# Eight experts on one core: x in two large loads, stores on the gpsimd ring, the last two gated to a weight piece

## The chip, the cores and the metric

The kernel runs on one core of a Trainium2 chip. The metric is the device time of one execution in microseconds, as the median of several runs. TensorE multiplies; VectorE (DVE) and ScalarE (ACT) empty its accumulators; GpSimd (POOL) and SyncE (SP) here mostly issue transfers. A transfer is carried by the core's 16 DMA engines, whichever engine issued it. Transfers issued by gpsimd and those issued by sync or scalar stand in different queues, called rings below. A transfer that changes the type (float32 to bfloat16) is issued by gpsimd in this kernel.

## What is computed

```
x:  8 experts x 256 rows x 512      w1: 8 x 512 x 2048      w2: 8 x 2048 x 512   (float32)
h = max(x @ w1, 0)
out = h @ w2                         8 x 256 x 512 float32
```

Each expert has two weights of 4.19 MB in float32. The 16 of them, 67.1 MB, are read once; x and the output are 4.19 MB each.

## The kernel before

All matmuls run in bfloat16. Weights are cast on the way in: each is one gpsimd DMA (L57 for w1, L63 for w2) into a tile of 128 partitions x 8192 elements, that is 32 KB of float32 in a row of DRAM per partition and 16 KB of bfloat16 in SBUF. The pool "weights" has four buffers for w1 and four for w2 (both are called w_sb in the profile). The w2 of the last two experts come in pieces: three for expert 6, seven for expert 7, the last three of them one k-slice each.

x comes expert by expert in float32 on the sync queue (L53): 128 partitions x 2 rows of 512, 4 KB per partition. Four experts are loaded ahead; expert e + 4 is loaded after the second layer of e. ACT casts it (L67), TensorE transposes it in eight 128x128 blocks (L73), and DVE evicts the blocks (L77). Cast and transposes of expert e + 1 stand inside the first layer of expert e.

A first layer is 64 matmuls per expert (L89) into eight accumulators, each emptied with a relu by DVE (L97) or ACT (L99) into ht. A second layer is 32 matmuls (L111) into two accumulators of 128x512, evicted by DVE (L119) and ACT (L120) into an output tile. The store of an expert is one 0.5 MB DMA on the sync queue (L125), as soon as both evictions are done; the last expert's goes out in two halves, on sync (L122) and scalar (L123).

The order is written out by hand: first and second layer of experts 0 to 4 in turn, then the first layers of 5, 6, 7, then their second layers. Weights are issued in the order of use, all from the gpsimd queue, which works in order: a weight whose buffer is still in use holds up everything behind it. A transfer on the gpsimd ring also waits for the eighth before it, since their completion is counted on eight semaphores in rotation.

Of the kernel before, what the change touches and what calls it, by code (L numbers as in the profile page):

```python
# [1 line left out]

# [5 lines left out]


@with_exitstack  # L10
def kernel(
    ctx: ExitStack,
    tc: tile.TileContext,
    x: bass.AP,
    w1: bass.AP,
    w2: bass.AP,
    out: bass.AP,
):
    nc = tc.nc
    P = 128  # L20
    bf = mybir.dt.bfloat16
    f32 = mybir.dt.float32

    E, C, H = x.shape
    F = w1.shape[2]
    MT = C // P
    KT1 = H // P
    KT2 = F // P
    AHEAD = 4


    x_r = x.rearrange("e (p mt) k -> e p mt k", p=P)
    w1_r = w1.rearrange("e (p kt) n -> e p kt n", p=P)
    w2_r = w2.rearrange("e (p kt) n -> e p kt n", p=P)
    out_r = out.rearrange("e (p mt) n -> e p mt n", p=P)

    const = ctx.enter_context(tc.tile_pool(name="const", bufs=1))
    wpool = ctx.enter_context(tc.tile_pool(name="weights", bufs=4))
    xpool = ctx.enter_context(tc.tile_pool(name="xs", bufs=AHEAD))
    tpool = ctx.enter_context(tc.tile_pool(name="xts", bufs=2))  # L40
    hpool = ctx.enter_context(tc.tile_pool(name="hidden", bufs=4))
    opool = ctx.enter_context(tc.tile_pool(name="outs", bufs=3))
    ps_h = ctx.enter_context(tc.tile_pool(name="ps_h", bufs=4, space=bass.MemoryType.PSUM))
    ps_o = ctx.enter_context(tc.tile_pool(name="ps_o", bufs=4, space=bass.MemoryType.PSUM))

    x_sb, xb, xt, w1_sb, w2_sb, ht = {}, {}, {}, {}, {}, {}


    ctx.enter_context(tc.manual_schedule())

    def load_x(e):
        x_sb[e] = xpool.tile([P, MT, H], f32, tag="x", name="x_sb")
        nc.sync.dma_start(x_sb[e][:], x_r[e])  # L53

    def load_w1(e):
        w1_sb[e] = wpool.tile([P, KT1, F], bf, tag="w1", name="w1_sb")
        nc.gpsimd.dma_start(w1_sb[e][:], w1_r[e])  # L57

    def load_w2(e):
        w2_sb[e] = wpool.tile([P, KT2, H], bf, tag="w2", name="w2_sb")  # L60
        cuts = {E - 2: (0, 6, 11, 16), E - 1: (0, 4, 8, 11, 13, 14, 15, 16)}.get(e, (0, KT2))
        for lo, hi in zip(cuts, cuts[1:]):
            nc.gpsimd.dma_start(w2_sb[e][:, lo:hi, :], w2_r[e, :, lo:hi, :])  # L63

    def cast_x(e):
        xb[e] = tpool.tile([P, MT, H], bf, tag="xb", name="x_bf")
        nc.scalar.copy(xb[e][:], x_sb[e][:])  # L67

    def transpose_x(e):
        pt = ps_o.tile([P, KT1, MT, P], bf, tag="ps_o", name="pt_tr")  # L70
        for kt in range(KT1):
            for mt in range(MT):
                nc.tensor.transpose(  # L73
                    pt[:, kt, mt, :], xb[e][:, mt, kt::KT1], identity[:]
                )
        xt[e] = tpool.tile([P, KT1, C], bf, tag="xt", name="xt_sb")
        nc.vector.tensor_copy(xt[e][:], pt[:].rearrange("p k m q -> p k (m q)"))  # L77

    def first_layer(e):
        if e + 1 < E:  # L80
            cast_x(e + 1)
        ht[e] = hpool.tile([P, KT2, C], bf, tag="ht", name="ht_sb")
        for g in range(KT2 // 2):
            if g == KT2 // 4 and e + 1 < E:
                transpose_x(e + 1)
            ph = ps_h.tile([P, 2, C], f32, tag="ps_h", name="pt_h")
            for i in range(2):
                for kt in range(KT1):
                    nc.tensor.matmul(  # L89
                        ph[:, i, :],  # L90
                        w1_sb[e][:, kt, 2 * g + i::KT2],
                        xt[e][:, kt, :],
                        start=(kt == 0),
                        stop=(kt == KT1 - 1),
                    )
            if g % 2:
                nc.vector.tensor_relu(ht[e][:, 2 * g:2 * g + 2, :], ph[:])  # L97
            else:
                nc.scalar.activation(  # L99
                    ht[e][:, 2 * g:2 * g + 2, :], ph[:],  # L100
                    mybir.ActivationFunctionType.Relu,
                )

    def second_layer(e):
        last = e == E - 1
        po = [
            ps_o.tile([P, H], f32, tag="ps_o", name=f"pt_o{mt}") for mt in range(MT)
        ]
        order = [(kt, mt) for kt in range(KT2) for mt in range(MT)]
        for kt, mt in order:  # L110
            nc.tensor.matmul(  # L111
                po[mt][:],
                ht[e][:, kt, mt * P:(mt + 1) * P],
                w2_sb[e][:, kt, :],
                start=(kt == 0),
                stop=(kt == KT2 - 1),
            )
        o = opool.tile([P, MT, H], f32, tag="o", name="out_sb")
        nc.vector.tensor_copy(o[:, 0, :], po[0][:])  # L119
        nc.scalar.copy(o[:, 1, :], po[1][:])  # L120
        if last:
            nc.sync.dma_start(out_r[e, :, 0, :], o[:, 0, :])  # L122
            nc.scalar.dma_start(out_r[e, :, 1, :], o[:, 1, :])  # L123
        else:
            nc.sync.dma_start(out_r[e], o[:])  # L125


    order = []
    for e in range(E - 3):
        order += [(1, e), (2, e)]  # L130
    order += [(1, e) for e in range(E - 3, E)] + [(2, e) for e in range(E - 3, E)]

    for e in range(AHEAD):
        load_x(e)
    for layer, e in order:
        (load_w1 if layer == 1 else load_w2)(e)
        if (layer, e) == (1, 0):
            identity = const.tile([P, P], bf, name="identity")
            make_identity(nc, identity)
    cast_x(0)  # L140
    transpose_x(0)
    for layer, e in order:
        if layer == 1:
            first_layer(e)
        else:
            second_layer(e)
            if e + AHEAD < E:
                load_x(e + AHEAD)


# [1 line left out]
_INS = ['x', 'w1', 'w2']  # L152
_OUTS = [((8, 256, 512), 'float32')]


# [23 lines left out]
```

## Time and profile before

| | |
|---|---|
| time, median of three (lowest, highest) | 185.76 us (185.62, 185.86) |
| span of the profiled run | 183.9 us |
| mean granted TensorE clock | 0.924 |
| gpsimd ring: packets, MB written | 3456, 33.56 |
| sync ring: packets, MB written | 2304, 8.13 |
| scalar ring: packets, MB written | 144, 0.26 |
| median from issue to landing: x load, store, 2 MB weight | 26.1, 16.1, 65.1 us |

The page of a profile has the busy time of each engine, a picture of the span in 40 slices, the DMA queues, the chain of work that ended last, the groups of instructions by line with what ended the idle time before them, and the DMA issues. The MB of a queue count what is written, so a weight that is read as 4.19 MB counts as 2.10 MB. Time of idle on an engine that is not the bottleneck costs nothing.

### The profile page before, as it was taken

To read this page: it belongs to the slowest core of one execution; us is meant where nothing else is said; L and a number is where in the kernel's file an instruction comes from. 1 tells how busy PE (TensorE), PEld (TensorE's weight loads), DVE (VectorE), ACT (ScalarE), POOL (GpSimd) and SP (SyncE) were. 2 spreads that over 40 slices of the span, in tenths; PEclk is the share of its full clock that TensorE was granted. 3 is DMA by queue.
4 is the path that set the end of the run, shared out by engine and by line. 5 is a ranking of instruction groups with operands and counts; after the bars stand their busy time and mean duration, and the time that the engine had idled before them with its cause. 6 is when DMAs were issued, how large, how long until landed. Compare 5 with 4: busy or idle time off the path is not lost.

```text
span 183.9 us, 1901 instructions
## 1 busy us (share of the span) xinstructions
PE 132.1 (72%) x832; PEld 91.9 (50%) x832; DVE 32.5 (18%) x48; ACT 32.8 (18%) x49; POOL 13.5 (7%) x30
## 2 busy tenths in 40 slices
PE   0204959579891996929987396865989595899980
PEld 0103954159640892317942385324889494344420
DVE  0100430104301141001411033010244333010101
ACT  3300220312103130021302212031143132010101
POOL 7300010100100001000040100101010010210000
PEclk9999999957999699985999979996699999999999
DMA  5999999989999999999999999999999999999973
GB/s 221 274 217 219 280 214 228 224 201 232 265 215 246 251 219 248 246 217 257 249 212 254 236 223 272 216 224 274 215 232 214 228 228 190 212 214 240 232 190 116
DMA packets 5912, 42.06 MB, mean 229 GB/s; under 512 B 656, under 2 KB 1040, under 8 KB 4112
## 3 DMA queue, kind: packets, MB, share of 16 engines
q0 software_dynamic: 3456, 33.56, 86.4%
q1 hardware_dynamic: 2304, 8.13, 11.7%
q10 hardware_dynamic: 144, 0.26, 0.4%
q8 instruction: 6, 0.10, 0.2%
q14 instruction: 2, 0.02, 0.0%
HBM read 71.30 MB, written 4.19 MB: 410 GB/s over the span
## 4 chain that ended last, share of the span: by engine, by line
another core or an unknown queue 38%; DMA 33%; PE 19%; POOL 4%; issue 3%; DVE 0%; POOLq 0%
DMA w_sb<-in_w_dram 33%; PE pt_h L89 10%; PE pt_o L111 8%; POOL w_sb L63 3%; POOL w_sb L57 1%; PE pt_tr L73 0%; DVE out_sb L119 0%; POOL identity masks.py:199 0%; POOL identity masks.py:197 0%; POOLq masks.py:199 0%; POOLq L174 0%; POOLq L63 0%; POOLq L163 0%
## 5 line engine op out<-in xcount | busy, mean ns | idle before, releaser
L89 PE MATMUL pt_h<-xt_sb,w_sb 128*128 128x256 bf16 x512 | 72.1, 310 | 31.2 <-DMA w_sb<-in_w_dram 31.2
L89 PEld LDWEIGHTS <-w_sb 128*128 128x128 bf16 x512 | 63.1, 150 | 40.3 <-DMA w_sb<-in_w_dram 34.4
L111 PE MATMUL pt_o<-w_sb,ht_sb 128*128 128x512 bf16 x256 | 57.0, 379 | 11.0 <-DMA w_sb<-in_w_dram 10.9
L111 PEld LDWEIGHTS <-ht_sb 128*128 128x128 bf16 x256 | 25.0, 98 | 41.6 <-issue 13.4
L97 DVE TENSOR_SCALAR ht_sb<-pt_h 128x512 bf16<-128x512 f32 x32 | 22.1, 692 | 80.0 <-PE pt_h L89 80.0
L99 ACT ACTIVATE ht_sb<-pt_h 128x512 bf16<-128x512 f32 x32 | 19.1, 597 | 75.9 <-PE pt_h L89 75.9
L120 ACT COPY out_sb<-pt_o 128x512 f32<-128x512 f32 x8 | 4.7, 586 | 68.5 <-PE pt_o L111 68.5
L119 DVE COPY out_sb<-pt_o 128x512 f32<-128x512 f32 x8 | 5.5, 691 | 61.7 <-PE pt_o L111 61.7
L63 POOL DMA_DIRECT2D w_sb<-in_w_dram x16 | 8.6, 540 | 73.6 <-DMA w_sb<-in_w_dram 65.1
L57 POOL DMA_DIRECT2D w_sb<-in_w_dram x8 | 4.4, 556 | 76.7 <-PE pt_h L89 75.9
L73 PE MATMUL pt_tr<-identity,x_bf 128*128 128x128 bf16 x64 | 5.3, 230 | 5.2 <-ACT x_bf L67 5.2
L67 ACT CAST x_bf<-x_sb 128x1024 bf16<-128x1024 f32 x8 | 8.4, 1046 | 2.3 <-DMA x_sb<-in_x_dram 2.3
L73 PEld LDWEIGHTS <-x_bf 128*128 128x128 bf16 x64 | 4.7, 116 | 5.2 <-ACT x_bf L67 5.2
L77 DVE COPY xt_sb<-pt_tr 128x1024 bf16<-128x1024 bf16 x8 | 5.5, 682 | 6.3 <-PE pt_tr L73 6.3
L67 ACT ACT_TABLE_LOAD x1 | 1.3, 1283 | 0.7 <-PEq L163 0.7
masks.py:199 POOL TENSOR_SCALAR_AFFINE_SELECT identity<-identity 128x128 bf16<-128x128 bf16 x1 | 0.3, 288 | 0.1
masks.py:197 POOL MEMSET identity<- 128x128 bf16 x1 | 0.2, 223 | 0.0
L163 POOL MEMSET const-float32-0.0<- 128x1 f32 x1 | 0.1, 98 | 0.2 <-issue 0.2
L163 POOL MEMSET const-bfloat16-1.0<- 128x1 bf16 x1 | 0.1, 102 | 0.0
L163 POOL MEMSET const-uint8-127<- 128x1 uint8 x1 | 0.1, 102 | 0.0
L163 POOL MEMSET const-float32-1.0<- 128x1 f32 x1 | 0.1, 98 | 0.0
## 6 DMA issues: line engine op xcount, KB each, us to landing
w_sb<-in_w_dram POOLq DMA_DIRECT2D x14, 2048.0 KB, 65.1
x_sb<-in_x_dram SPq DMA_DIRECT2D x8, 512.0 KB, 26.1
out_dram<-out_sb SPq DMA_DIRECT2D x7, 512.0 KB, 16.1
w_sb<-in_w_dram POOLq DMA_DIRECT2D x2, 640.0 KB, 65.6
w_sb<-in_w_dram POOLq DMA_DIRECT2D x2, 512.0 KB, 49.6
w_sb<-in_w_dram POOLq DMA_DIRECT2D x1, 768.0 KB, 66.6
w_sb<-in_w_dram POOLq DMA_DIRECT2D x1, 384.0 KB, 37.1
w_sb<-in_w_dram POOLq DMA_DIRECT2D x3, 128.0 KB, 17.8
```

Of the source, the lines that this page charges most:

```text
L57: nc.gpsimd.dma_start(w1_sb[e][:], w1_r[e])
L63: nc.gpsimd.dma_start(w2_sb[e][:, lo:hi, :], w2_r[e, :, lo:hi, :])
L67: nc.scalar.copy(xb[e][:], x_sb[e][:])
L73: nc.tensor.transpose(pt[:, kt, mt, :], xb[e][:, mt, kt::KT1], identity[:])
L77: nc.vector.tensor_copy(xt[e][:], pt[:].rearrange("p k m q -> p k (m q)"))
L89: nc.tensor.matmul(ph[:, i, :], w1_sb[e][:, kt, 2 * g + i::KT2], xt[e][:, kt, :], start=(kt == 0), stop=(kt == KT1 - 1),)
L97: nc.vector.tensor_relu(ht[e][:, 2 * g:2 * g + 2, :], ph[:])
L99: nc.scalar.activation(ht[e][:, 2 * g:2 * g + 2, :], ph[:], mybir.ActivationFunctionType.Relu,)
L111: nc.tensor.matmul(po[mt][:], ht[e][:, kt, mt * P:(mt + 1) * P], w2_sb[e][:, kt, :], start=(kt == 0), stop=(kt == KT2 - 1),)
L119: nc.vector.tensor_copy(o[:, 0, :], po[0][:])
L120: nc.scalar.copy(o[:, 1, :], po[1][:])
L163: nc = _bacc.Bacc("TRN2", target_bir_lowering=False, num_devices=1)
```

## The change

x is read in two loads of four experts each, with eight rows of 512 (16 KB) per partition. The first comes in float32 on the sync queue and is cast by ACT in four pieces; the second is cast on the way by a gpsimd DMA that stands between the weights of expert 1. Each group is transposed at once: the first before any matmul, the second inside the first layer of expert 2, a quarter after every second accumulator. Since partition p now holds eight successive rows, the eviction of the transposes puts columns back in order with a strided pattern, shared between DVE and ACT.

The weights get three buffers of each kind instead of four, which makes room for the x tiles and five output tiles.

The stores of experts 0 to 4 are issued by gpsimd, each at a place chosen among the weights; the queue then carries, in order: w1 3, w2 3, store 0, w1 4, w2 4, store 1, w1 5, w1 6, w1 7, w2 5, store 2, w2 6, store 3, store 4, w2 7. The stores of 5 and 6 stay on sync, but wait until the third last piece of the last weight has landed; they are meant to keep out of the way of the last weights. The stores on gpsimd and the long rows of x are meant to keep small packets from standing between those of the weights.

```diff
-    AHEAD = 4
-    x_r = x.rearrange("e (p mt) k -> e p mt k", p=P)
+    G = 2
+    EG = E // G
+    J = EG * C // P
+    WB = 3
+    x_r = x.rearrange("(g e) c k -> g (e c) k", g=G).rearrange(
+        "g (p j) k -> g p j k", p=P
+    )
...
-    wpool = ctx.enter_context(tc.tile_pool(name="weights", bufs=4))
+    wpool = ctx.enter_context(tc.tile_pool(name="weights", bufs=WB))
+    hpool = ctx.enter_context(tc.tile_pool(name="hidden", bufs=3))
+    opool = ctx.enter_context(tc.tile_pool(name="outs", bufs=5))
...
+    def transpose_x(g, kts):
+        for kt in kts:
+            pt = ps_o.tile([P, J, P], bf, tag="ps_o", name="pt_tr")
+            for j in range(J):
+                nc.tensor.transpose(pt[:, j, :], x_b[g][:, j, kt::KT1], identity[:])
...
+                if mt % 2:
+                    nc.scalar.copy(dst, src[:, mt])
+                else:
+                    nc.vector.tensor_copy(dst, src[:, mt])
...
+    def store(e):
+        nc.gpsimd.dma_start(out_r[e], o_sb[e][:])
+
+    nc.sync.dma_start(x_f[:], x_r[0])
+    load_w1(0)
+    make_identity(nc, identity)
+    load_w2(0)
+    load_w1(1)
+    nc.gpsimd.dma_start(x_b[1][:], x_r[1])
+    load_w2(1)
+    load_w1(2)
+    load_w2(2)
+    for j in range(0, J, 2):
+        nc.scalar.copy(x_b[0][:, j:j + 2, :], x_f[:, j:j + 2, :])
+    transpose_x(0, range(KT1))
+
+    first_layer(0)
+    load_w1(3)
+    second_layer(0)
+    load_w2(3)
+    store(0)
+    first_layer(1)
+    load_w1(4)
+    second_layer(1)
+    load_w2(4)
+    store(1)
+    first_layer(2, [lambda kt=kt: transpose_x(1, [kt]) for kt in range(KT1)])
+    load_w1(5)
+    second_layer(2)
+    first_layer(3)
+    load_w1(6)
+    second_layer(3)
+    first_layer(4)
+    load_w1(7)
+    load_w2(5)
+    store(2)
+    load_w2(6)
+    store(3)
+    second_layer(4)
+    store(4)
+    load_w2(7)
...
+    for e in (5, 6):
+        d = nc.sync.dma_start(out_r[e], o_sb[e][:])
+        tc.add_manual_dep(
+            d.ins,
+            pieces[-3].ins.name,
...
+            reason="after the weights",
+        )
+    nc.sync.dma_start(out_r[7, :, 0, :], o_sb[7][:, 0, :])
+    nc.scalar.dma_start(out_r[7, :, 1, :], o_sb[7][:, 1, :])
```

## The prediction

> **What bounds the kernel now.** I read the page from the engine shares to the queues, then the TensorE timeline, then the DMA answers for single stretches. On the page, TensorE is busy 72% of the span, while the DMA line has a 9 in nearly every slice:
>
> ```profile
> PE 132.1 (72%) x832; PEld 91.9 (50%) x832; DVE 32.5 (18%) x48; ACT 32.8 (18%) x49; POOL 13.5 (7%) x30
> ...
> DMA  5999999989999999999999999999999999999973
> ...
> HBM read 71.30 MB, written 4.19 MB: 410 GB/s over the span
> L89 PE MATMUL pt_h<-xt_sb,w_sb 128*128 128x256 bf16 x512 | 72.1, 310 | 31.2 <-DMA w_sb<-in_w_dram 31.2
> ```
>
> The first-layer matmuls wait 31.2 us, all of it for weights. So the DMA engines bound the kernel, and a change is worth what it takes off their work, or adds to it, ahead of the last weight. The starts in the TensorE timeline are then landing times of weights, wherever the idle time in brackets is put down to a DMA:
>
> ```profile
> 16.44 5.18 PE L89 MATMUL pt_h<-xt_sb,w_sb 128*128 128x256 bf16 x32 [10.15 <-DMA w_sb<-in_w_dram]
> ...
> 37.92 6.36 PE L89 MATMUL pt_h<-xt_sb,w_sb 128*128 128x256 bf16 x32 [3.35 <-DMA w_sb<-in_w_dram]
> ...
> 126.11 6.64 PE L89 MATMUL pt_h<-xt_sb,w_sb 128*128 128x256 bf16 x32 [3.42 <-DMA w_sb<-in_w_dram]
> ...
> 137.15 3.72 PE L89 MATMUL pt_h<-xt_sb,w_sb 128*128 128x256 bf16 x32 [0.46 <-DMA w_sb<-in_w_dram]
> ...
> 146.94 7.21 PE L89 MATMUL pt_h<-xt_sb,w_sb 128*128 128x256 bf16 x64 [2.13 <-DMA w_sb<-in_w_dram]
> 157.08 18.86 PE L111 MATMUL pt_o<-w_sb,ht_sb 128*128 128x512 bf16 x86 [2.93 <-DMA w_sb<-in_w_dram]
> ```
>
> From 37.92 to 126.11 eight weights land, and beside them eight half-megabyte transfers of the sync ring (about four stores and four x loads): 88.19 us, 11.02 us per pair. From 137.15 to 157.08 two weights land with next to nothing beside them: 19.93 us, **w = 10.0 us** each (an earlier one without company, 27.5 to 37.9, is near it at 10.2 once its first store packets are taken off). A half-megabyte on the sync ring therefore costs **u = 1.0 us**, less than its bytes at the weights' rate (0.524 MB at 4.194 MB per 10.0 us: 1.25 us). In rates: 428 GB/s where both rings work, 420 where only the gpsimd ring does. The DMA queue part for two such stretches, 16 to 27 us and then 27.5 to 36 us (queue: packets, MB, share), shows why:
>
> ```profile
> q0 software_dynamic: 144, 2.10, 89.2%
> q1 hardware_dynamic: 144, 0.52, 12.6%
> ...
> q0 software_dynamic: 111, 1.82, 100.3%
> ```
>
> In the first, 144 packets of each ring went in 11 us: one small packet after each large one, with shares summing to over 100%, so that they overlap a little.
>
> **The end.** The last weight piece lands at 178.96 (chain of waits). Two matmuls, a 0.69 us eviction, a store issued at 180.60 that lands 2.4 us later, and the close: 183.9, a tail of 4.94 us. The reported time is 1.86 us above the span. The last pieces, from the w_sb tile's issue-to-landing times: the third of expert 6 is issued at 104.17 and takes 62.2 us (166.4), the last of expert 7 at 163.59 and takes 15.4 us (179.0). Expert 6's w2 so took 9.4 us with no store in progress; expert 7's took 12.6 us with the stores of 5 and 6 in it.
>
> **What the Trainium skill says.** All from "DMA: Bandwidth & Descriptors". (1) Section "Queues, rings and completion order": each DMA engine goes round robin over the rings that have work, a packet at a time. The 144 against 144 packets agree. (2) "Issuing engines are not separate DMA queues": all rings share the 16 engines, so another ring gives no bandwidth. The trace agrees but for 2% (428 against 420). (3) "Anatomy of one DMA — SWDGE (gpsimd) path": the semaphore write at a DMA's end is nearly free. No run here isolates it: w is 0.36 us above what 435 GB/s, the ceiling in "Where 436 GB/s comes from", would give (9.64).
>
> **The change, part by part.**
>
> *Start.* x of experts 0-3 is one 2 MB load instead of four of 0.5 MB; same bytes, same ring. Before, the fourth x load landed 25.5 us after its issue, at about 27.6, so that at 16.4, when the first weight landed, one unit of u was still owed. If rows of 16 KB travel as larger packets they get a larger share against the 32 KB weight rows and all of x is in when the first weight is: 16.4 + 0.8 = 17.2. If they travel as 4 KB packets, x comes later and the weight earlier; the work done is the same. TensorE starts later: four casts of 1.05 us (row L67) and 32 transposes with eight evictions before the first matmul, some 8 us after x. I cost this at nothing: TensorE idles 31 us for first-layer weights and needs about 16 us per expert, where DMA needs 20.
>
> *Buffers, four to three per kind.* The fourth w1 now waits for expert 0's first layer. With x at 15 to 28 us, that ends at 31 to 45; the ring then holds weights until about 72 (17.2 + 5w + x). Nothing starves. On the gpsimd queue stand, behind that wait, w2 of 3, store 0, w1 of 4 and so on in order; a store there waits for an eviction and holds up the next weight. The narrowest places I worked through (weights of 6 issued at 89 with the ring filled to 122; w1 of 7 and w2 of 5 issued after expert 4's first layer at 110, filled to 132; w2 of 7 at 142, behind a wait for w1 of 7, filled to 165) all keep 20 us or more. Cost nothing.
>
> *x of experts 4-7* comes with a cast on the gpsimd ring: 2.1 MB read, half a weight's bytes: 5.0 us, where four units on the sync ring cost 4.0. Adds 1.0. Removes four casts on ACT, which were hidden.
>
> *Stores 0-4 on the gpsimd ring*, s each, where the sync ring paid 1.0. The trace has no store on that ring. Lower bound: u, 1.0. By bytes at 420 GB/s: 1.25. The last 0.53 MB, alone at the end (181.2 to 182.65), took 1.45. With a gap for the close of a DMA (w less 9.64: 0.36) on top: 1.7 or so. I take the byte price, 1.25, since the first x packets, alone at 2.4 to 4 us, moved at 410 to 450 GB/s: rows of 4 KB are no slower than rows of 32. Five times 0.25 adds 1.25.
>
> *Stores 5 and 6* wait for the third last piece, so 1.05 MB leaves the stretch before the last weight. Expert 7's w2 goes from 12.6 to 10.0 us: takes 2.6. They start at about 1 us after the gate opens (the first byte of the final stores came 0.9 us after issue), hence as the last piece lands, need 2.6 us and are through at T + 2.5, where the last stores put out their first byte. I add 0.1 to the tail.
>
> *Sum.* 17.2 + 13 weights at 10.0 + 5.0 + 5 x 1.25 + 9.4 (w2 of 6) + 10.0 (w2 of 7) = 177.85 for the last piece. The same prices give the kernel before 16.4 + 13 x 10.0 + 10 x 1.0 + 9.4 + 12.6 = 178.4, which is 0.56 short of the measured 178.96; so I trust the difference, -0.55, not the sum, and put the last piece at 178.4. (By terms: start -0.2, x +1.0, stores +1.25, gate -2.6.) TensorE doesn't hold it back: w2 of 5 lands at some 153, and three second layers need 96 matmuls at 0.221, 21.2 us. Span 178.4 + 4.94 + 0.1 = 183.45; time **185.3 us**, 0.25% faster: a small difference of large terms.
>
> **Rivals.** *A, only bytes count.* The mean rate to the last piece is 74.97 MB in 176.9 us, 424 GB/s; if it holds, with 1.05 MB less ahead of the last weight (2.5 us), the time is 183.4. For it: the DMA line is full throughout. Against: 420 where one ring works alone. *B, the gpsimd ring pays for each store and its close.* s = 1.5: 1.25 us more, 186.55, slower than before; at s = 1.7 187.55. For it: within one large DMA, packets come 1.21 us apart, 9.7 for eight, so 0.3 is lost between DMAs, which another ring's packets used to fill. Against: the ten pieces of the last two weights show no such loss. *C, the ring runs dry*, three buffers and blocked stores: if x took 44 us (32 rounds of 1.375, a packet of each ring), first layer 0 would end at 63, still 9 us ahead of the ring's end; over 188 only if I misjudge the start.
>
> **How the numbers follow.** Forecast 0.45 (185.3, plus or minus 0.7, for w between 9.9 and 10.1), A 0.22, B 0.28, C 0.05. The range runs from A's 183.4, rounded down, to 187.1, inside B; B's upper end and C are left out. No change is 185.4 to 186.1, which holds about a third of the forecast and a little of B: 0.17. Slower is the rest of B and C, 0.30. Faster is A and the rest of the forecast: 0.53.
>
> **What would show it.** TensorE idle put down to DMA before each layer, with the DMA line full, means the ring never ran dry. Queue q1 should fall to x and three stores, q0 rise. Landing intervals with only a weight should be 10.0; those with a store in them 11.25 (11.0 for A, 11.5 or more for B). w2 of 7 should take 10 us, not 12.6, and the last piece land at 178.4. A gap in the DMA line in the middle, or TensorE waiting for transposes after 40 us, would make C right and me wrong.

## The result, and the profile after

| kernel | median, us | lowest to highest | ratio to before (95% interval) |
|---|---|---|---|
| before | 185.81 | 185.62 to 186.24 | 1 |
| changed | 183.69 | 183.55 to 184.13 | 0.9887 (0.9862 to 0.9912) |

The change takes 2.1 us off; the forecast was 0.5 us (185.3), and rival A, "only bytes count", had said 183.4. First the page of the changed kernel: the DMA line, queues q0 (gpsimd) and q1 (sync) with packets, MB written and share, and the group of first-layer matmuls with what ended its idle time.

```profile
DMA  5999999999999999999999999999999999999976
...
q0 software_dynamic: 4320, 37.23, 93.9%
q1 hardware_dynamic: 576, 3.41, 5.0%
...
HBM read 71.30 MB, written 4.19 MB: 415 GB/s over the span
...
L97 PE MATMUL pt_h<-xt,w_sb 128*128 128x256 bf16 x512 | 63.8, 288 | 19.5 <-DMA w_sb<-in_w_dram 18.6
```

The megabytes read and written are what they were, and the DMA line is full from its second slice on: the ring never ran dry, with three buffers and with stores in gpsimd's queue. The 576 packets of q1 are four transfers of 128 packets of data and 16 small ones that close a transfer: the stores of 5 and 6, half of the last store, and the float32 x. The 2.1 MB of x in 128 packets are 16 KB each, so rows of 16 KB do travel as 16 KB packets.

The TensorE timeline (start, length, what, and in brackets the idle time before it and who ended it) gives the landings of the weights w1 of 5, 6, 7 and w2 of 5, then of the first and second piece of w2 of 7:

```profile
124.28 7.21 PE L97 MATMUL pt_h<-xt,w_sb 128*128 128x256 bf16 x64 [3.87 <-DMA w_sb<-in_w_dram]
133.99 7.21 PE L97 MATMUL pt_h<-xt,w_sb 128*128 128x256 bf16 x64 [2.50 <-DMA w_sb<-in_w_dram]
143.64 7.21 PE L97 MATMUL pt_h<-xt,w_sb 128*128 128x256 bf16 x64 [2.43 <-DMA w_sb<-in_w_dram]
153.34 15.55 PE L117 MATMUL pt_o<-w_sb,ht_sb 128*128 128x512 bf16 x64 [2.49 <-DMA w_sb<-in_w_dram]
169.31 1.90 PE L117 MATMUL pt_o<-w_sb,ht_sb 128*128 128x512 bf16 x8 [0.42 <-DMA w_sb<-in_w_dram]
171.76 5.71 PE L117 MATMUL pt_o<-w_sb,ht_sb 128*128 128x512 bf16 x24 [0.56 <-DMA w_sb<-in_w_dram]
```

The three weights behind the first, without company, land 9.71, 9.65 and 9.70 us apart, where I had used 10.0. And w2 of expert 5 lands at 153.3, before at 157.0. The end of the chain of waits (start, length, what):

```profile
165.92 10.92 DMA w_sb<-in_w_dram
176.84 0.04 issue
```

The last piece lands at 176.84 instead of 178.96 (2.1 us earlier). The span is 181.8, the tail thus 5.0, as before.

What a store costs on the gpsimd ring is read from three neighbours in that ring: the issue times in gpsimd's timeline, and the time from issue to landing in the answers for the tiles w_sb, out_sb and w_sb.

```profile
35.72 0.53 POOL L71 DMA_DIRECT2D w_sb<-in_w_dram  x1 [6.38 <-PE pt_o L117]
36.53 0.54 POOL L129 DMA_DIRECT2D out_dram<-out_sb  x1 [0.29 <-issue]
45.28 0.53 POOL L62 DMA_DIRECT2D w_sb<-in_w_dram  x1 [8.21 <-PE pt_h L97]
...
DMA to landing us min/median/max: 57.0/57.0/57.0
...
DMA to landing us min/median/max: 57.5/57.5/57.5
...
DMA to landing us min/median/max: 58.4/58.4/58.4
```

35.72 + 57.0 = 92.7; 36.53 + 57.5 = 94.0; 45.28 + 58.4 = 103.7. The store took 1.3 us of the ring, the weight behind it 9.7: together 11.0, rival A's figure, where my prices had 11.25. The other four stores came 1.2 to 1.3 after what stood ahead of them. The bfloat16 x landed at 42.6, 4.9 us after the weight before it.

### The profile page after: what moved, and what is told of

It reads as the page before. It is cut to its first block, busy times and chain, and to the rows that moved or that the text cites. A ratio compares the mean times of both kernels' runs of the same rounds, so it can differ in the third digit from the quotient of the medians.

```text
span 181.8 us, 1885 instructions
## 1 busy us (share of the span) xinstructions
PE 129.8 (71%) x832; PEld 89.5 (49%) x832; DVE 32.8 (18%) x48; ACT 33.4 (18%) x53; POOL 16.7 (9%) x36
## 4 chain that ended last, share of the span: by engine, by line
DMA 59%; PE 29%; another core or an unknown queue 5%; POOL 3%; issue 1%; ACT 0%; POOLq 0%
DMA w_sb<-in_w_dram 59%; PE pt_h L97 15%; PE pt_o L117 13%; POOL w_sb L71 1%; PE pt_tr L80 1%; POOL w_sb L62 1%; ACT out_sb L126 0%; POOL out_dram L129 0%; POOL x_b L137 0%; POOL identity masks.py:199 0%; POOL identity masks.py:197 0%; POOLq masks.py:199 0%; POOLq L215 0%; POOLq L204 0%
## 5 line engine op out<-in xcount | busy, mean ns | idle before, releaser
L97 PE MATMUL pt_h<-xt,w_sb 128*128 128x256 bf16 x512 | 63.8, 288 | 19.5 <-DMA w_sb<-in_w_dram 18.6
L97 PEld LDWEIGHTS <-w_sb 128*128 128x128 bf16 x512 | 58.9, 147 | 25.0 <-DMA w_sb<-in_w_dram 21.6
L117 PE MATMUL pt_o<-w_sb,ht_sb 128*128 128x512 bf16 x256 | 61.0, 398 | 11.9 <-DMA w_sb<-in_w_dram 11.8
L117 PEld LDWEIGHTS <-ht_sb 128*128 128x128 bf16 x256 | 25.9, 102 | 45.4 <-issue 18.7
L80 PE MATMUL pt_tr<-identity,x_b 128*128 128x128 bf16 x64 | 6.5, 262 | 16.3 <-ACT x_b L142 16.3
L80 PEld LDWEIGHTS <-x_b 128*128 128x128 bf16 x64 | 5.3, 128 | 17.0 <-ACT x_b L142 17.0
L89 DVE COPY xt<-pt_tr 128x512 bf16<-128x512 bf16 x8 | 5.5, 686 | 18.3 <-PE pt_tr L80 18.2
L142 ACT CAST x_b<-x_f 128x1024 bf16<-128x1024 f32 x4 | 3.9, 1042 | 11.5 <-DMA x_f<-in_x_dram 11.5
L87 ACT COPY xt<-pt_tr 128x512 bf16<-128x512 bf16 x8 | 4.7, 586 | 6.9 <-DVE xt L89 6.7
L129 POOL DMA_DIRECT2D out_dram<-out_sb x5 | 2.7, 540 | 17.8 <-DMA w_sb<-in_w_dram 17.2
```

The lines of the kernel that those rows point to most:

```text
L80: nc.tensor.transpose(pt[:, j, :], x_b[g][:, j, kt::KT1], identity[:])
L87: nc.scalar.copy(dst, src[:, mt])
L89: nc.vector.tensor_copy(dst, src[:, mt])
L97: nc.tensor.matmul(ph[:, i, :], w1_sb[e][:, kt, 2 * g + i::KT2], xt[e // EG][:, kt, e % EG, :], start=(kt == 0), stop=(kt == KT1 - 1),)
L117: nc.tensor.matmul(po[mt][:], ht[e][:, kt, mt * P:(mt + 1) * P], w2_sb[e][:, kt, :], start=(kt == 0), stop=(kt == KT2 - 1),)
L142: nc.scalar.copy(x_b[0][:, j:j + 2, :], x_f[:, j:j + 2, :])
```

## The experiments

Three parts can be taken apart: the gate on stores 5 and 6, the ring (and place) of stores 0 to 4, and x with its buffers. They were run alone, then in pairs, and then place against ring. All times are medians, beside runs of the kernel before on the same chip.

### The gate alone

```diff
+        elif e in (E - 3, E - 2):
+            d = nc.sync.dma_start(out_r[e], o[:])
+            tc.add_manual_dep(
+                d.ins,
+                pieces[-3].ins.name,
...
         else:
             nc.sync.dma_start(out_r[e], o[:])
```

> The kernel before, with only the stores of experts 5 and 6 gated to the third last weight piece. Bytes theory (what counts is the megabytes ahead of the last piece): 1.05 MB less there, last piece about 2.4 us earlier, time 183.4. Rival (TensorE takes over the end): w2 of expert 5 still lands at about 157.0, and 96 matmuls at 0.221 us need 21.2 us from there, so the last matmul can end no earlier than about 178.3 against 179.6; time 184.5 to 185.1, with TensorE no longer waiting for the last pieces.

Measured: 184.34 us, ratio 0.9924 (0.9896 to 0.9953). Its TensorE timeline at the end:

```profile
156.72 20.88 PE L115 MATMUL pt_o<-w_sb,ht_sb 128*128 128x512 bf16 x96 [0.81 <-DMA w_sb<-in_w_dram]
```

All 96 second-layer matmuls run in one piece, with no wait from 156.72 to 177.6. The last piece landed at 176.4, 2.5 us earlier than before, so the 2.6 us that the prediction gave the gate are there in the transfers. But TensorE got through only at 177.6, and the last stores were issued at 178.29 and 178.61, 1.8 and 2.2 us after the last piece instead of 1.3 and 1.6. The time falls by 1.5. The rival's mechanism holds, its range (184.5 to 185.1) was a little too high: the gate pays only until TensorE sets the end.

### The ring of stores 0 to 4 alone

```diff
-        else:
+        elif e > 4:
             nc.sync.dma_start(out_r[e], o[:])
...
+    def store(e):
+        nc.gpsimd.dma_start(out_r[e], o_sb[e][:])
...
+    load_w1(7)
+    load_w2(5)
+    store(2)
+    load_w2(6)
+    store(3)
```

> The kernel before, with only the stores of experts 0 to 4 moved to the gpsimd ring, at the places of the changed kernel; x, four weight buffers and the ungated stores of 5 and 6 as before. Prices of the prediction (10.0 us a weight, a store 1.0 us on the sync ring and 1.25 on the gpsimd ring): stores 2 to 4 move from ahead of w2 of expert 5 to behind it, the last piece 1.2 us later, time 186 to 187. Rival (a store costs 1.3 us on either ring, a weight 9.7 where no 4 KB packets run beside it): the same bytes, 0 to 1 us less, 184.8 to 185.8.

Measured: 186.08 us, ratio 1.0005 (0.9990 to 1.0019). By the time alone, this lies just inside the range of the prices (186 to 187) and 0.3 above the rival's. The landing decides: the last piece came at 179.1 (before 179.0), so the 1.2 us more that the prices gave did not come. Both kernels have the same bytes ahead of that piece, and they take the same time on either ring, as the rival said, though it named up to 1 us less. Two things come with the edit: five output tiles instead of three, and x of experts 4 to 7 is issued earlier (the fifth load at 5.1 us instead of 35.6), since no store stands ahead of it on the sync queue.

### x and the three buffers alone

```diff
     def store(e):
-        nc.gpsimd.dma_start(out_r[e], o_sb[e][:])
+        nc.sync.dma_start(out_r[e], o_sb[e][:])
...
     for e in (5, 6):
-        d = nc.sync.dma_start(out_r[e], o_sb[e][:])
-        tc.add_manual_dep(
...
+        nc.sync.dma_start(out_r[e], o_sb[e][:])
```

> The changed kernel with all stores of experts 0 to 6 on the sync ring as soon as they are ready, so that only x in two loads and the three weight buffers remain of the change. Prices of the prediction: start -0.2, x of experts 4-7 +1.0, so 186.6. Rival (the form of the x loads sets how the 16 DMA engines stand to each other, and with them out of step a weight takes 9.7 instead of 10.0 us): some 15 weights at up to 0.3 less, 183 to 185, and weights without company land 9.7 us apart.

Measured: 185.84 us, ratio 1.0000 (0.9989 to 1.0010). Both theories missed: neither my +0.8 nor a gain. The form of x and the three buffers together are worth nothing; what each does by itself was not measured.

### The changed kernel with x in 4 KB packets

```diff
-    nc.sync.dma_start(x_f[:], x_r[0])
+    for j in range(0, J, 2):
+        nc.sync.dma_start(x_f[:, j:j + 2, :], x_r[0][:, j:j + 2, :])
```

> The changed kernel with its first x load cut into four sync loads of 4 KB per partition, everything else the same (same SBUF layout, same bytes). Packet theory (16 KB packets at the start put the engines out of step, which makes a weight 9.7 us): weights go back to 10.0 us, in-step bursts with empty slices between them come back in the DMA line, time 185 to 187. Rival (the packet size of x does nothing later on; the sync ring only starts faster with four issues, 0.77 MB in the first 4 us against 0.56): 183.0 to 183.7, weights still 9.7 us.

Measured: 183.86 us, ratio 0.9893 (0.9870 to 0.9916), against 0.9887 for the changed kernel. The three weights without company landed 9.7, 9.8 and 10.0 us apart; the last was late, and the store behind it made that up (1.0 us instead of 1.3). The time did not go to 185 or more, so the packet theory falls. The rival is right on the size of the packets (its range, 183.0 to 183.7, is 0.2 too low), but not on a faster start: 0.49 MB went in the first 4 us, less than with one load (0.56), and x was complete at 28.8 instead of 13.5. Neither matters to the end.

### Both store parts, without x

```diff
 # ring_stores_alone, and for experts 5 and 6:
+            tc.add_manual_dep(
+                d.ins,
+                pieces[-3].ins.name,
...
```

> The kernel before with both store parts of the change (stores 0 to 4 on the gpsimd ring, 5 and 6 gated), x and four weight buffers as before. Theory now (a 2 MB weight costs 9.7 us and a half-megabyte 1.3 us on either ring, so x in two loads gains nothing; the gate pays in full once w2 of expert 5 lands early enough for TensorE): the whole change without its x part, 183.3 to 183.9, w2 of expert 5 at about 153. Rival (the x part is needed, through the 4 KB packets that otherwise stand between the weights): no better than the gate alone, 184.3.

Measured: 183.67 us, ratio 0.9891 (0.9871 to 0.9911). That is the whole gain of the change without its x part, and w2 of expert 5 landed at 152.8, as the theory said (153). TensorE started on it at once:

```profile
152.86 13.97 PE L115 MATMUL pt_o<-w_sb,ht_sb 128*128 128x512 bf16 x62 [0.83 <-DMA w_sb<-in_w_dram]
```

### The gate and x, stores 0 to 4 back on sync

```diff
     def store(e):
-        nc.gpsimd.dma_start(out_r[e], o_sb[e][:])
+        nc.sync.dma_start(out_r[e], o_sb[e][:])
```

> The changed kernel with stores 0 to 4 on the sync ring as soon as they are ready; gate of 5 and 6, x and buffers as changed. Theory now: stores 2 to 4 again stand ahead of w2 of expert 5, which lands at about 157, and TensorE, with 21 us of second layers from there, sets the end: 184.1 to 184.6, as the gate alone. Rival (where stores 0 to 4 stand is of no matter, each costs 1.3 us anywhere ahead of the last piece): 183.7 as the changed kernel.

Measured: median 185.69, ratio 0.9968 (0.9947 to 0.9989). The median misses both ranges. The 22 executions fall into two groups, 7 between 183.8 and 184.3, near the theory's 184.1 to 184.6, and 15 from 185.4 up. The profiled one, 186.1, belongs to the second. Its TensorE timeline from w2 of expert 5 on, and busy times by stretch (engine columns, then the granted TensorE clock, DMA share and GB/s):

```profile
157.12 22.57 PE L117 MATMUL pt_o<-w_sb,ht_sb 128*128 128x512 bf16 x94 [2.98 <-DMA w_sb<-in_w_dram]
```

```profile
157.00:162.00 5.00, 4.83 (x14) 1.89 (x15) 0.00 (x0) 0.00 (x0) 1.06 (x2) 0.66 1.04 213
162.00:167.00 5.00, 5.00 (x24) 2.25 (x23) 0.69 (x1) 0.58 (x1) 0.53 (x1) 1.00 1.05 213
```

The weights were all in at 176.3; TensorE ended at 179.7. Its clock was 0.66 on average from 157 to 162, and 14 matmuls ran where the next 5 us hold 24. Closer in, it was 0.50 from 158.5 to 161.7. In the 20.9 us that the run with the gate alone needed for the same matmuls, it would have ended 1.7 us earlier, which makes 184.4, near the first group. That each of the other longer executions had such a stretch is inferred; only this one was traced, and the mean clock of a whole execution doesn't tell the groups apart (0.92 to 0.95 in both). Why the gate alone came out long in only one of its six executions (185.63) is open. Now the same answer for the changed kernel:

```profile
153.00:157.00 4.00, 3.66 (x10) 1.35 (x10) 0.00 (x0) 0.00 (x0) 1.06 (x2) 0.57 1.04 223
```

It too met a low clock, 0.57, at the start of its second layers. With w2 of 5 in at 153.3 it had the time to make it up and still waited for pieces of expert 7.

### The ring and x, without the gate

```diff
-        d = nc.sync.dma_start(out_r[e], o_sb[e][:])
-        tc.add_manual_dep(
...
+        nc.sync.dma_start(out_r[e], o_sb[e][:])
```

> The changed kernel without the gate: stores 5 and 6 go out on sync as soon as they are ready. Theory now: the bytes of these two stores (2 x 1.3 us) come back ahead of the last piece, 185.6 to 186.2, as before. Rival (x and ring stores help together though neither does alone): 184.5 to 185.

Measured: 185.93 us, ratio 1.0010 (0.9995 to 1.0025); last piece at 179.14. As the theory said: without the gate nothing is gained. The 22 executions spread from 185.2 to 187.6, and no trace shows why.

### The gate two pieces earlier

```diff
-            pieces[-3].ins.name,
+            pieces[-5].ins.name,
```

> The changed kernel with the stores of 5 and 6 gated to the fifth last piece instead of the third last, so that they start some 2 us earlier, where the DMA line of the changed kernel falls to 2 to 4 tenths (175 to 176.5 us). If engines that have finished their share of the last pieces take up the stores: the last piece stays at 176.8 and the stores are out of the way of the last ones, 183.2 to 183.6. If the stores' packets stand between those of the last pieces: the last piece 1 us later, 184.3 to 184.8.

Measured: 183.66 us, ratio 0.9882 (0.9866 to 0.9898), last piece at 176.46. The stores took the engines that had run empty (from 172 to 177 the DMA share is 1.11, with the changed kernel 0.80) and did not hold up the last pieces. Yet nothing was gained over the changed kernel (183.69): there the halves of the last store already took only 2.2 and 2.75 us from issue to landing, here 2.0 and 2.6. The first theory holds, though its 183.2 to 183.6 was a little too low.

### Place or ring

```diff
     def store(e):
-        nc.gpsimd.dma_start(out_r[e], o_sb[e][:])
+        d = nc.sync.dma_start(out_r[e], o_sb[e][:])
+        if e >= 2:
+            tc.add_manual_dep(
+                d.ins,
+                pieces[5].ins.name,
...
+                reason="after w2 of expert 5",
```

> The changed kernel with stores 0 to 4 on the sync ring: 0 and 1 as soon as they are ready, 2 to 4 held until w2 of expert 5 has landed; gate of 5 and 6 as changed. It has the place of the changed kernel's stores without its ring. If place is what counts (w2 of expert 5 at 153 instead of 157, so that TensorE has some 4 us to spare at the end): 183.5 to 184.0, in a narrow spread. If the ring counts: 184 to 186 in a wide one, as with all five stores on sync as soon as they are ready.

Measured: 183.48 us (183.37 to 183.57), ratio 0.9868 (0.9849 to 0.9888). TensorE from w2 of expert 5 on:

```profile
153.05 0.58 PE L117 MATMUL pt_o<-w_sb,ht_sb 128*128 128x512 bf16 x1 [2.97 <-DMA w_sb<-in_w_dram]
153.85 23.06 PE L117 MATMUL pt_o<-w_sb,ht_sb 128*128 128x512 bf16 x93 [0.22 <-issue]
```

The weight lands at 153.0 again, though all stores are on sync. TensorE met a low clock here as well (0.58 us for the first matmul) and ran through to 176.9, just after the last piece at 176.28, so that it cost little. It is the place of stores 2 to 4, behind w2 of expert 5, that helps; in this kernel the ring they use is of no account.

### More stores in the tail

```diff
 # as gate_and_ring_stores, but
-    store(3)                           # second kernel only
-    store(4)
...
+    for e in (4, 5, 6):                # second kernel: (3, 4, 5, 6)
+        d = nc.sync.dma_start(out_r[e], o_sb[e][:])
+        tc.add_manual_dep(
+            d.ins,
+            pieces[-5].ins.name,
...
```

> The kernel before with its x and four weight buffers, stores 0 to 3 on the gpsimd ring, and the stores of 4, 5 and 6 on sync, gated to the fifth last piece. Prices: another half-megabyte leaves the stretch before the last piece (1.3 us) and fills DMA engines that run empty at 175 to 176.5, but comes back behind the last piece, where stores and the final halves then need 2.1 MB: 0 to 0.7 us less than with the change, 183.0 to 183.7. Rival (the packets of three stores stand between those of the last pieces): last piece no earlier than 176.3, 183.7 to 184.5.

> The same with the stores of 3 to 6 on sync, gated to the fifth last piece. If total bytes over the span set the end and the engines are kept busy, as with three: 183.0 to 183.7. If the final halves queue behind the stores on the sync ring: their issue to landing grows from 2.3 to over 3 us and the time goes up, 183.7 to 184.7.

Measured: 183.49 us, ratio 0.9871 (0.9851 to 0.9891), last piece at 175.1; and 183.01 us, ratio 0.9844 (0.9824 to 0.9864), last piece at 174.0. The second is the best kernel of the study, 0.7 us under the changed one. Its busy times by stretch:

```profile
172.00:174.00 2.00, 1.97 (x10) 0.78 (x8) 0.00 (x0) 0.00 (x0) 0.00 (x0) 1.00 1.13 361
174.00:176.00 2.00, 0.59 (x2) 0.10 (x1) 0.69 (x1) 0.59 (x1) 0.00 (x0) 1.00 1.02 416
176.00:178.00 2.00, 0.00 (x0) 0.00 (x0) 0.00 (x0) 0.00 (x0) 0.00 (x0) 1.00 1.02 412
```

The last halves waited behind the other stores, as the second theory said (4.9 us from issue to landing, not 2.3), and still the time fell: the DMA engines now have no gap from the last weights to the last store, where the changed kernel's share is 0.80 from 172 to 177.

## Why the prediction was right, and where it was off

**The range and the forecast**: 183.69 lies inside the stated range only because the range reached down to rival A. My own forecast, 185.3 plus or minus 0.7, was 1.6 too high, outside its own margin: 0.25% faster was measured as 1.1%. The direction was right, but it came out of terms of which three (start, x, stores) were off by 0.7 to 1.3 us.

**What bounds the kernel**: right. DMA bounds it in all the kernels, except at the end of those with the gate but with w2 of 5 at 157, where TensorE took over.

**The price of a weight, w = 10.0, and with it u = 1.0**: this is the step that was mis-sized. I took w from two landings of one trace, 9.79 and 10.14. In the run with the gate alone, which is the same program up to that point, the same two came 9.61 and 9.69 apart, and in the changed kernel 9.65 and 9.70. With w = 9.7, the 11.02 us of a weight and a half-megabyte leave u = 1.3 for the latter, not 1.0. I had defined u as the remainder, so the error in w went into it whole.

The trace of before already held the answer. gpsimd issues each of these pieces 0.28 us after the landing for which it waits, so that its issues show the landings. First two lines of before, then four of the gate alone:

```profile
157.32 0.53 POOL L63 DMA_DIRECT2D w_sb<-in_w_dram  x1 [9.61 <-DMA w_sb<-in_w_dram]
160.55 0.53 POOL L63 DMA_DIRECT2D w_sb<-in_w_dram  x1 [2.70 <-DMA w_sb<-in_w_dram]
...
137.66 0.53 POOL L66 DMA_DIRECT2D w_sb<-in_w_dram  x1 [10.56 <-DMA w_sb<-in_w_dram]
147.27 0.53 POOL L66 DMA_DIRECT2D w_sb<-in_w_dram  x1 [9.08 <-DMA w_sb<-in_w_dram]
156.96 0.53 POOL L66 DMA_DIRECT2D w_sb<-in_w_dram  x1 [9.16 <-DMA w_sb<-in_w_dram]
160.66 0.53 POOL L66 DMA_DIRECT2D w_sb<-in_w_dram  x1 [3.18 <-DMA w_sb<-in_w_dram]
```

Before, w2 of 5 took 10.14 us and the next piece, six of the 16 k-slices of w2 of 6, took 3.23; with the gate alone it was 9.69 and 3.70. Both make 13.4 us for 22 slices, which is 9.7 for a weight. So the 10.14 was one late landing that the next piece made up at once. The 9.4 that I used for w2 of 6 is the other side of it (9.8 with the gate alone). And 9.7 for the eight packets of a weight stood in the prediction, where I gave it to rival B.

Left open: w1 and w2 of expert 3 in the changed kernel's trace took 10.5 and 10.4 us with nothing beside them (10.0 and 9.7 with x in 4 KB packets), and nothing made that up, though the DMA engines were as busy then as after it (share 1.01 from 71.78 to 92.68, 1.00 from 93.99 to 113.30). Single landings scatter by up to 1 us between these runs, and no run shows why. So the sums don't come out: w = 9.7 and u = 1.3 give 16.4 + 14 x 9.7 + 10 x 1.3 + 12.6 = 177.8 for the last piece of before (measured 178.96), and 18.3 + 14 x 9.7 + 4.9 + 5 x 1.3 + 10.0 = 175.5 for that of the change (176.84): the first weight, 14 more up to w2 of 6, the half-megabytes and x, then w2 of 7. The prices explain the difference, not the whole.

**Stores on the gpsimd ring, +1.25, and x of 4-7, +1.0**: these two terms were that error. s = 1.25 was right (1.2 to 1.3 measured), and x took 4.9 us for my 5.0, but the sync ring had been paying 1.3 for each half-megabyte as well. The stores then come to 0 and x to -0.3, which fits the runs with each part alone (ratios 1.0005 and 1.0000).

**The start, -0.2**: the first weight landed at 18.3, not 17.2, and the second at 28.0, before at 27.5: +0.5. Less of x had moved in the first 4 us (0.56 MB, before 0.77); at the 424 GB/s of rival A the missing 0.21 MB is 0.5 us, by an estimate.

**The gate, -2.6**: -2.5 in the run with the gate alone. By terms the last piece comes out at +0.5 - 0.3 + 0 - 2.5 = -2.3, measured -2.1; my sum had -0.55.

**TensorE "doesn't hold it back"**: right for the whole change: w2 of 5 landed at 153.3, with 21.2 us of matmuls from there. That I wrote "some 153" was luck, since my own prices gave 17.2 + 13 x 10.0 + 5.0 + 2 x 1.25 = 154.7; TensorE would have kept up with that too. What I didn't see is that this is the use of moving stores 2 to 4. I counted their ring as a cost; their place is worth the 0.7 us between the gate alone and the gate with them, and more where the clock is low.

**The tail, +0.1**: not there. From the last piece to the end of the span it was 5.0 us before and 4.9 with the change.

**Rivals.** A was nearest (183.4 for 183.69), and its argument stands: bytes ahead of the last piece count, whichever ring moves them. The 2% between the two rings that spoke against it came from one late landing. B's loss between DMAs isn't there (a store took 1.2 to 1.3 us, not 1.5 to 1.7), and C did not occur: fourth w1 issued at 28.8, with the ring filled to 72.

## What to carry to other kernels

Where one resource is full throughout, ask of each transfer not which queue carries it but what stands behind it: in this kernel half a megabyte cost 1.3 us on either ring, and it came cheaper only where the engines would else run empty, here behind the last load. When that load comes earlier, look at the next engine in line from its last big wait to the end, with room for a low clock. And a price that is the small remainder of two large ones needs more than two samples, each read together with what lands next: its error is the whole error of the large one.

## What was not expected of the hardware

The TensorE clock stood at 0.50 for some 3 us just where the second layers of 5 to 7 began (158.5 to 161.7 in the traced run of the gate with x, 153.2 to 156.4 in the changed kernel), where TensorE had waited 3.0 and 2.5 us for a weight just before. Such stretches are in every trace, and where DMA sets the end they cost nothing: before has them at about 37, 61, 81, 105 and 125 us, each beside a wait of 3.35 to 3.93 us for a weight, but the changed kernel has one after a wait of 2.5 us and none after one of 3.87, so the waits alone don't tell where. Where TensorE sets the end, this is the one cause seen for executions of one program that differ by 2 us.

Packets of 4 KB on one ring between weight rows of 32 KB on the other took 1.3 us a half-megabyte, as on the one ring alone, little more than their bytes at the weights' rate (0.524 MB at 4.194 MB per 9.7 us: 1.2).
